# RWKV-7 block of a two-layer trunk: coupling, bonus and output products at other places of TensorE's fixed order, copies and small factors on ScalarE

## The chip, the core and the metric

The kernel runs on one core of a Trainium2 chip. The metric is the device time of one execution in microseconds (us), here the median over the runs shown. Five engines work side by side and are joined by semaphores: PE (TensorE, the matrix products), DVE (VectorE), ACT (ScalarE), POOL (GpSimd) and SP (SyncE, which only issues transfers). Each engine executes its own instructions strictly in the order in which they stand. An instruction that waits therefore holds up all that stand behind it on its engine, whether these wait for anything or not. This is the key to the whole change: nearly all it does is to alter such orders.

## What is computed

The reference is a trunk of two layers on x of 512 rows and 1024 columns, in f32. Each layer is half a SwiGLU feed-forward net, a mixer, and half a feed-forward net again. The mixer of layer 0 is attention and that of layer 1 is RWKV-7 time mixing, the only part that concerns us:

```python
xr, xw, xk, xv, xa, xg = [h + xx * mix[i] for i in range(6)]
r = (xr @ w_r).astype(f32)
k = (xk @ w_k).astype(f32)
v = (xv @ w_v).astype(f32)
...
def rwkv7_step(state, inp):
    r_t, w_t, k_t, v_t, a_t, b_t = inp
    sa = jnp.einsum('bhvk,bhk->bhv', state, a_t)
    state = (state * w_t[:, :, None, :] + sa[..., None] * b_t[:, :, None, :]
             + v_t[..., None] * k_t[:, :, None, :])
    return state, jnp.einsum('bhvk,bhk->bhv', state, r_t)
...
y = ((y - mu) * lax.rsqrt(var + GN_EPS)).reshape(B, S, D)
y = y * lnx_g.astype(f32) + lnx_b.astype(f32)
y = y + (jnp.sum(r_h * k_h * r_k.astype(f32), axis=-1, keepdims=True) * v_h).reshape(B, S, D)
return (y.astype(h.dtype) * g) @ w_o
```

There are 16 heads of 64 columns. The term with r_k is the "bonus": a sum over each head of r times k, spread over the head again and multiplied with v.

## The kernel before

**Products.** Every f32 operand of a large product is split into a high and a low part, and each product is made of three matmuls (mm3). All of them go through one helper line, L112 of the kernel, so that in the profile they are told apart by the tile they write: `rm` is a bank of the projections of k, v and r, `rq` a bank for small products (decay, coupling, sums over heads and their spread, transposes), `rr` and `ra` are the recurrence's, `wo` the output product's and `b` the feed-forward net's. These tiles lie in PSUM, from which an engine must have copied a bank before TensorE may fill it anew.

**The recurrence** does not step through time. The 512 positions fall into 8 chunks of 64, and within a chunk the steps are solved together, which needs the inverse of a triangular matrix for each head and chunk. The 16 heads are two groups of 8 ("group 0" and "group 1"). For each group `rw_own_ties` makes the products inside 32-position blocks, `rw_inverse` inverts these blocks, and its coupling steps (small 32x32 products) join two blocks to one of 64. Then `rw_recur` goes through the 8 chunks one after the other, each depending on the state that the last one left.

**The inverse** is a chain on VectorE: 31 pairs of a product and an add (L1376, L1380 before; L1379 and L1384 in the changed file), each over all blocks of the group at once. Its input `lin` is loaded from DRAM by SP; its result is copied by ScalarE (L1384 before, L1388 after, 128x1024, called "U" here) and goes with T out to DRAM (`tout`) and back in another layout, as the coupling steps need it.

**What sets the order.** A scheduler places the instructions of every engine, by costs and data, but inside the recurrent block `self.pinned` is set: each TensorE instruction is chained to the one before it, so TensorE follows the order in which the program writes them. That order is written out by hand. The functions are generators that stop ("yield") at places where other work may be put in, and `weave(main, (steps, side), ...)` goes through the main one and, after its n-th stop, takes one step of each side whose list names n. A projection `project` has 8 stops: after each of the first six k groups, then after each pair of banks with the last two k groups. `rw_recur` has 24, three for each chunk. Behind the block `pinned` is false and the scheduler places TensorE's instructions too; with `self.gate` an instruction can be put behind another in that order.

**Before**, the first half of r's projection carries the decay of group 1 in steps 0 to 3, the coupling of group 0's inverse in 2 to 5 and group 1's keys in 3 to 6. The second half carries the bonus sums (`rw_prep2`) and group 1's ties. The recurrence of group 0 carries the bonus sums of the second half (3, 4) and the coupling of inverse(1) (16, 17, 19, 20). The recurrence of group 1 carries the post-processing `rw_post(0)` of group 0, in which v is loaded back from DRAM (`vd`), transposed (L1567 on TensorE) and multiplied with the spread bonus; and the scheduler fills it with the output products of group 0's columns. `rw_post(1)` and the output products of group 1 follow, then the last feed-forward net.

## Time and profile before

| | us |
|---|---|
| three runs | 2158.67, 2158.33, 2158.3 |
| median | 2158.33 |
| the profiled execution | 2159.79 |
| its span | 2157.7 |
| recurrent block from r's projection to the last output product (timeline) | 1383 to 1794 |
| PE, DVE, ACT, POOL busy | 2071.5, 1166.8, 777.4, 168.1 |

The profile is one execution. Its own time stands 1.46 us over the median and 2.09 over its span, so sums made on the trace are brought to the median by taking off 1.46. In timeline rows the columns are start, duration, engine, line, operation, output and inputs, shapes, count, and in brackets how long the engine had been idle and what released it. A group of matmuls in one row is a run of them back to back. The granted clock is the share of full speed that TensorE was given, averaged over the stretch.

### The profile page before, as it was taken

The page shows a single profiled execution, that of the slowest core. Times are in us where ns is not written, and L with a number is a line of the kernel's source. Part 1 is how long each engine was busy: PE and PEld are TensorE (multiplying, and loading weights), DVE is VectorE, ACT ScalarE, POOL GpSimd, SP SyncE. Part 2 cuts the span into 40 slices and gives each one's busy share as a digit, 9 for nine tenths or more (in the row PEclk, how much of TensorE's full clock was granted, in tenths as well). Part 3 has the DMA queues.
Part 4 walks back from the last instruction along what each step waited for, and adds up shares of the span by engine and source line. Part 5 has one row for each costly group of instructions (what it writes and reads, how often), then busy time and mean ns, then how long its engine had stood idle before and what let it go on. Part 6 is the DMA issues. An engine that isn't in the chain of part 4 may idle for free.

```text
span 2157.7 us, 28358 instructions
## 1 busy us (share of the span) xinstructions
PE 2071.5 (96%) x11407; PEld 1665.8 (77%) x11407; DVE 1166.8 (54%) x1608; ACT 777.4 (36%) x1177; POOL 168.1 (8%) x193
## 2 busy tenths in 40 slices
PE   8999999999989999999999999998678989999999
PEld 6888887767878888888888888766456758888887
DVE  5444444367777544547445445676764545444443
ACT  4222223355335332335333333463314334222222
POOL 2000001011010000002000000123222101000000
PEclk9999999999989999999999999999799999999999
DMA  5232323331118656565554654447343332232331
GB/s 179 78 110 86 108 87 108 103 88 40 50 55 266 205 166 195 161 200 188 168 191 151 187 171 159 175 150 244 101 115 100 96 117 87 81 115 92 99 103 59
DMA packets 261915, 282.36 MB, mean 131 GB/s; under 512 B 45011, under 2 KB 221291, under 8 KB 261784
## 3 DMA queue, kind: packets, MB, share of 16 engines
q1 hardware_dynamic: 259672, 278.46, 41.7%
q10 hardware_dynamic: 2112, 2.10, 0.3%
q8 instruction: 89, 1.46, 0.3%
q14 instruction: 42, 0.34, 0.0%
HBM read 227.76 MB, written 54.59 MB: 131 GB/s over the span
## 4 chain that ended last, share of the span: by engine, by line
PE 90%; DVE 6%; DMA 2%; ACT 1%; issue 1%; SPq 0%; POOL 0%; ACTq 0%; DVEq 0%; POOLq 0%
PE b L112 67%; PE am L112 7%; PE rm L112 4%; PE rq L112 2%; PE wo L112 2%; PE rr L112 2%; PE rl L112 1%; DVE const L1376 1%; DVE const L1380 1%; DVE rec L873 1%; DMA parts<-parts 1%; PE an L695 0%; PE ad L852 0%; PE au L764 0%; DMA most<-const 0%
## 5 line engine op out<-in xcount | busy, mean ns | idle before, releaser
L112 PE MATMUL b<-xg,parts 128*128 128x512 f32 x4224 | 966.9, 390 | 0.7 <-ACT xg L395 0.7
L112 PEld LDWEIGHTS b<-xg,parts 128*128 128x128 f32 x4224 | 793.8, 188 | 168.0 <-issue 1.7
L268 DVE TENSOR_TENSOR parts<-const,parts 128x1024 fp32r<-128x1024 f32 (+1 forms) x320 | 362.8, 1141 | 303.0 <-ACT parts L267 302.4
L112 PE MATMUL b<-act,parts 128*128 128x512 f32 x2112 | 482.8, 389 | 0.0
L267 ACT CAST parts<-const 128x1024 fp32r<-128x1024 f32 (+1 forms) x320 | 312.1, 977 | 458.9 <-PE b L112 394.8
L112 PEld LDWEIGHTS b<-act,parts 128*128 128x128 f32 x2112 | 396.0, 188 | 82.1
L383 POOL TENSOR_TENSOR ssum<-ssum,sq 128x512 f32<-128x512 f32 x42 | 65.3, 1555 | 1205.6 <-DVE const L508 340.6
L508 DVE SCALAR_TENSOR_TENSOR const<-b,const 128x512 f32<-128x512 f32 x128 | 87.4, 687 | 107.5 <-PE b L112 107.5
L301 ACT CAST act<-u 128x512 fp32r<-128x512 f32 x88 | 54.7, 622 | 248.0 <-DVE u L494 248.0
L493 DVE TENSOR_TENSOR u<-b,rstd 128x512 f32<-128x512 f32 x88 | 60.5, 691 | 148.4 <-PE b L112 148.2
L94 ACT ACTIVATE g<-g 128x512 f32<-128x512 f32 x88 | 55.1, 630 | 189.7 <-DVE g L488 189.7
L488 DVE TENSOR_TENSOR g<-b,rstd 128x512 f32<-128x512 f32 x88 | 60.3, 689 | 94.9 <-PE b L112 94.6
L112 PE MATMUL am<-xg,parts 128*128 128x512 f32 x384 | 99.6, 411 | 0.2 <-ACT xg L395 0.2
L112 PEld LDWEIGHTS am<-xg,parts 128*128 128x128 f32 x384 | 72.4, 192 | 25.3 <-issue 9.4
L302 DVE TENSOR_TENSOR act<-u,act 128x512 fp32r<-128x512 f32 x88 | 60.6, 689 | 36.9 <-ACT act L301 36.4
L494 DVE TENSOR_TENSOR u<-u,g 128x512 f32<-128x512 f32 x88 | 60.5, 692 | 2.7
L112 PE MATMUL rm<-xm,parts 128*128 128x512 f32 x252 | 60.8, 394 | 0.0
L219 DVE TENSOR_TENSOR pparts<-praw,pparts 128x1024 fp32r<-128x1024 f32 (+2 forms) x37 | 42.9, 1163 | 29.1 <-ACT pparts L218 29.0
L112 PEld LDWEIGHTS rm<-xm,parts 128*128 128x128 f32 x252 | 46.6, 188 | 12.7 <-issue 3.2
L218 ACT CAST pparts<-praw 128x1024 fp32r<-128x1024 f32 (+2 forms) x37 | 36.9, 1003 | 53.3 <-DMA praw<-in_rw_wv_dram 13.0
L112 PE MATMUL wo<-z,parts 128*128 128x512 f32 x192 | 49.2, 401 | 2.2 <-ACT z L301 1.9
L112 PE MATMUL am<-parts,xg 128*128 128x512 f32 x192 | 47.5, 402 | 0.0
(261 smaller groups left out, 1729.2 us busy)
## 6 DMA issues: line engine op xcount, KB each, us to landing
const<-in_ffn_w_gate_dram SPq DMA_DIRECT2D x88, 512.0 KB
const<-in_ffn_w_up_dram SPq DMA_DIRECT2D x88, 512.0 KB
parts<-pparts SPq DMA_DIRECT2D x68, 512.0 KB
parts<-parts SPq DMA_DIRECT2D x68, 512.0 KB
const<-in_ffn_w_down_dram SPq DMA_DIRECT2D x64, 512.0 KB
const<-in_ffn_w_down_dram SPq DMA_DIRECT2D x48, 256.0 KB
const<-in_attn_w_in_dram SPq DMA_DIRECT2D x16, 512.0 KB
lora<-pparts SPq DMA_DIRECT2D x8, 576.0 KB
```

Of the source, the lines that this page charges most:

```text
L94: ins = nc.scalar.activation(out, in_, func, **kw)
L112: return self.pe(self.nc.tensor.matmul(*args, **kw))
L219: nc.vector.tensor_tensor(out=lo, in0=src, in1=hi.bitcast(F32), op=ALU.subtract)
L267: self.nc.scalar.copy(hi[:r, :n], raw[:, :n])
L268: self.lo_engine.tensor_tensor(out=lo[:r, :n], in0=raw[:, :n], in1=hi[:r, :n].bitcast(F32), op=ALU.subtract)
L301: self.nc.scalar.copy(hi, t)
L302: self.nc.vector.tensor_tensor(out=lo, in0=t, in1=hi.bitcast(F32), op=ALU.subtract)
L383: nc.gpsimd.tensor_tensor(out=ssum, in0=ssum, in1=sq, op=ALU.add)
L488: nc.vector.tensor_tensor(out=g, in0=ps[i], in1=rstd, op=ALU.mult)
L493: nc.vector.tensor_tensor(out=u, in0=ps[2 + i], in1=rstd, op=ALU.mult)
L494: nc.vector.tensor_tensor(out=u, in0=u, in1=gs[i], op=ALU.mult)
L508: nc.vector.scalar_tensor_tensor(out=self.x[c], in0=ps, scalar=0.5, in1=self.x[c], op0=ALU.mult, op1=ALU.add)
```

## The change

Six things are altered. (1) In r's projection the decay moves from steps 0 to 3 of the first half to 2 to 5, group 1's keys go to 6, 7 and, of the second half, 0, 1; the coupling of inverse(0) moves to steps 2 to 5 of the second half, the ties to 4 to 7, the bonus sums to 6, 7. (2) In the recurrence of group 0 the bonus sums move from 3, 4 to 6, 7 and the coupling of inverse(1) from 16, 17, 19, 20 to 18, 19, 21, 22. (3) The load of `vd`, its transposes and the bonus product leave `rw_post` for a generator of their own, `rw_bonus`; the recurrence of group 1 carries `rw_bonus(0)`, `rw_post(0)` and, in steps 15 to 19, `rw_bonus(1)`, which stood behind the recurrence before. (4) The output products of group 0 are put behind the last TensorE instruction of the recurrence of group 1. (5) r's four banks are copied to SBUF by ScalarE and VectorE reads the copies; the bank with the head sums is copied by ScalarE instead of VectorE. (6) Three kinds of small operations go from VectorE to ScalarE: the factor 1/C of the means of v (8 of 128x8), the addition of 1 in the decay (8 of 128x512), the factor -2 of each chunk's first column (8 of 128x8). The inverse's load from DRAM is no longer held back by the masks; its first VectorE operation is.

```diff
+        weave(project(0, None, evac_r, False, 0), ((2, 3, 4, 5), decay), ((6, 7), keys))
         weave(
-            project(0, None, evac_r, False, 0),
-            ((0, 1, 2, 3), decay), ((2, 3, 4, 5), inverse), ((3, 4, 5, 6), keys),
+            project(1, None, evac_r, False, 0),
+            ((0, 1), keys), ((2, 3, 4, 5), inverse), ((4, 5, 6, 7), ties), ((6, 7), bonus[0]),
         )
-        weave(project(1, None, evac_r, False, 0), ((0, 1), bonus[0]), ((0, 1, 2, 3), ties))
...
-        weave(recur, ((3, 4), bonus[1]), ((16, 17, 19, 20), inverse))
+        weave(recur, ((6, 7), bonus[1]), ((18, 19, 21, 22), inverse))
...
-        post = self.rw_post(0)
-        recur = self.rw_recur(1)
-        weave(recur, ((1, 2, 4, 5, 7, 8, 10, 11, 13, 14), post))
-        for _ in post:
-            pass
+        plus, post, more = self.rw_bonus(0), self.rw_post(0), self.rw_bonus(1)
+        weave(
+            self.rw_recur(1),
+            ((0, 2, 3, 4, 6), plus), ((1, 3, 4, 5, 7, 8, 10, 11, 13, 14), post), ((15, 16, 17, 18, 19), more),
+        )
+        done = self.last_pe
         self.pinned = False
         self.fetch_x(self.rr[1, 2])
-        self.rw_out(self.z)
+        self.rw_out(self.z, done)
...
-                nc.vector.tensor_scalar(out=mean, in0=mean, scalar1=1.0 / C, scalar2=None, op0=ALU.mult)
+                nc.scalar.mul(mean, mean, 1.0 / C)
...
-            nc.vector.tensor_scalar(out=pi, in0=pi, scalar1=1.0, scalar2=None, op0=ALU.add)
+            nc.scalar.activation(pi, pi, AF.Identity, bias=self.const(1.0))
...
-        for j, r in enumerate(rs):
+        rows = self.t("r", [4, S])
+        for j, ps in enumerate(rs):
+            nc.scalar.copy(rows[:, j, :], ps)
+        for j in range(4):
             m = 4 * sg + j
-            t, rp = rw["k"][m], self.plane(sg, j, 1)
+            t, r, rp = rw["k"][m], rows[:, j, :], self.plane(sg, j, 1)
...
-            nc.vector.tensor_copy(y, ps)
+            nc.scalar.copy(y, ps)
...
-        load = self.after(nc.sync.dma_start(L, rw["lin", sg]), dep)
+        load = nc.sync.dma_start(L, rw["lin", sg])
...
+            if i == 0:
+                self.after(ins, dep)
...
+    def rw_bonus(self, sg):
+        nc = self.nc
+        self.plus = [self.plane(0, j, 4) for j in range(4)]
+        vns = [self.plane(0, j, 1) for j in range(4)]
+        for j in range(4):
+            m = 4 * sg + j
+            src = self.rw["vd"][:, :, m * P : (m + 1) * P].rearrange("b p d -> p b d")
+            nc.sync.dma_start(vns[j].rearrange("p (b d) -> p b d", b=4), src)
+        yield
+        for j, (vn, t) in enumerate(zip(vns, self.plus)):
+            pv = self.bank("rq", 3)
+            for b in range(4):
+                self.pe(nc.tensor.transpose(pv[:, b * P : (b + 1) * P], vn[:, b * P : (b + 1) * P], self.ident))
+            nc.scalar.copy(t, pv)
+            pb = self.head_spread("b", 4 * sg + j)
+            nc.vector.tensor_tensor(out=t, in0=t, in1=pb, op=ALU.mult)
+            yield
...
-    def rw_out(self, z, late=4, dep=None):
+    def rw_out(self, z, dep=None):
         nc = self.nc
+        self.gate = dep
         for cb in range(4):
             w = self.next_w()
-            self.gate = dep if cb >= late else None
```

**TensorE, r's projection, around the first coupling step, before.** `rm` with 12 is one k group (or two banks of the last two k groups), `rq<-hids,parts` a decay piece, `rq<-const,heads 32x32` and `rq<-heads,const 32x32` the four coupling steps, `rq<-hids` the spread of a key norm.

```order
L112 MATMUL rm<-xm,parts 128x512 x12
L112 MATMUL rq<-hids,parts 128x512 x6
L112 MATMUL rm<-parts 128x512 x12
L112 MATMUL rq<-hids,parts 128x512 x6
L112 MATMUL rq<-const,heads 32x32 x32
L112 MATMUL rm<-parts 128x512 x12
L112 MATMUL rq<-hids,parts 128x512 x6
L112 MATMUL rq<-const,heads 32x32 x32
L112 MATMUL rq<-hids 128x512
L112 MATMUL rm<-xm,parts 128x512 x12
L112 MATMUL rq<-heads,const 32x32 x32
```

And in the change, where the rows begin with the end of the first half (its last two bank pairs with the first two spreads of keys) and lead into the second half; `rq<-heads 64x64` are the ties.

```order
L112 MATMUL rq<-hids 128x512
L112 MATMUL rm<-parts 128x512 x12
L112 MATMUL rq<-hids 128x512
L112 MATMUL rm<-parts 128x512 x12
L112 MATMUL rq<-hids 128x512
L112 MATMUL rm<-xm,parts 128x512 x12
L112 MATMUL rq<-const,heads 32x32 x32
L112 MATMUL rm<-parts 128x512 x12
L112 MATMUL rq<-const,heads 32x32 x32
L112 MATMUL rm<-parts 128x512 x12
L112 MATMUL rq<-heads,const 32x32 x32
L112 MATMUL rq<-heads 64x64 x16
```

The first coupling step stood behind the third k group of the first half; now it stands behind the third k group of the second half, with eight groups of rm products, four key spreads and a decay piece in between.

**ScalarE, the same place.** Before, the copy of the finished inverse (128x1024) stood between the last exponential of a decay piece and the coupling's copies:

```order
L94 ACTIVATE heads<-heads 128x512 x2
L1110 CAST xm<-const 128x512
L1292 ACTIVATE heads<-pa,const 128x512
L1384 COPY const<-const 128x1024
L1411 COPY const<-rq 32x512
L1110 CAST parts<-const 128x512
```

In the change, two pieces. The first is the decay: `heads<-rq` is a tanh that empties a bank, `heads<-heads 128x512 x2` are two exps that take in VectorE's scan.

```order
L94 ACTIVATE heads<-rq,const 128x512
L94 ACTIVATE pa<-rq,const 128x512
L1270 ACTIVATE heads<-heads,const 128x512
L1099 ACTIVATE const<-const 128x512
L94 ACTIVATE heads<-heads 128x512 x2
L1110 CAST parts<-const 128x512
L1110 CAST xm<-const 128x512
L94 ACTIVATE heads<-rq,const 128x512
```

The second is the copies of r's banks (L1338) with the copy of the inverse (L1388).

```order
L94 ACTIVATE heads<-heads 128x512 x2
L1338 COPY r<-rm 128x512
L1270 ACTIVATE heads<-heads,const 128x512
L1099 ACTIVATE const<-const 128x512
L1388 COPY const<-const 128x1024
L1338 COPY r<-rm 128x512
L1293 ACTIVATE heads<-pa,const 128x512
L1338 COPY r<-rm 128x512
L1110 CAST parts<-const 128x512
L1338 COPY r<-rm 128x512
```

One copy of a bank stands ahead of the inverse's copy, and three behind it.

**TensorE, the end of the recurrence of group 1, before.** `wo` are output products, `rr` and `ra` the recurrence, L1567 the transposes of v, `rq<-heads,const 8x512` sums over heads.

```order
L112 MATMUL rr<-recur,heads 64x64 x8
L112 MATMUL wo<-z,parts 128x512 x16
L112 MATMUL rr<-recur,heads 64x64 x8
L112 MATMUL wo<-z,parts 128x512 x21
L112 MATMUL rr<-am,bs 64x64 x8
L112 MATMUL rr<-heads,recur 64x64 x8
L112 MATMUL wo<-z,parts 128x512 x3
L112 MATMUL rq<-heads,const 8x512
L1567 MATMUL rq<-const,heads 128x128 x4
```

And in the change:

```order
L112 MATMUL rr<-recur,heads 64x64 x16
L112 MATMUL rr<-am,bs 64x64 x8
L112 MATMUL rr<-heads,recur 64x64 x8
L112 MATMUL wo<-z,parts 128x512 x24
L112 MATMUL rq<-heads,const 8x512 x4
L112 MATMUL rq<-hids,parts 128x512 x3
L112 MATMUL wo<-z,parts 128x512 x24
L112 MATMUL rq<-hids,parts 128x512
```

All output products now stand behind the recurrence, and group 1's sums stand between them; the transposes of v are gone from this place, into the recurrence.

More of the change, by code (lines that the diff above doesn't have):

```diff
@@ L1298, in rw_keys @@
             )
[L1299 to L1301 removed]
+            nc.scalar.mul(ar[:, 0, :, 0:1], ar[:, 0, :, 0:1], -2.0)
             nc.gpsimd.tensor_copy(self.pend[:, sg, j, :, None], ar[:, 1, :, C - 1 : C])
```

27 lines of the change are left out of this document (6 added, 21 removed).

## The prediction

> **What bounds the kernel now.** The page comes first: which engine fills the span, and where its row of slices dips.
>
> ```profile
> span 2157.7 us, 28358 instructions
> PE 2071.5 (96%) x11407; PEld 1665.8 (77%) x11407; DVE 1166.8 (54%) x1608; ACT 777.4 (36%) x1177; POOL 168.1 (8%) x193
> PE   8999999999989999999999999998678989999999
> PEclk9999999999989999999999999999799999999999
> ```
>
> TensorE is busy for 96% of the span. Its one long dip is slices 28 to 33, which is the recurrent block. So I cut that block at its own seams, read from TensorE's timeline further down, and asked for the engines' busy time in each piece (columns: length; busy time of PE, PEld, DVE, ACT, POOL; granted clock; DMA share; GB/s).
>
> ```profile
> 1380.00:1480.00 100.00, 100.00 (x526) 72.44 (x524) 64.05 (x96) 57.21 (x94) 22.35 (x22) 1.00 0.52 155
> 1491.37:1587.98 96.61, 68.72 (x613) 49.31 (x611) 70.22 (x123) 34.13 (x52) 28.72 (x25) 0.84 0.48 138
> 1587.98:1662.97 74.99, 53.99 (x1309) 43.88 (x1308) 42.29 (x96) 26.63 (x65) 13.38 (x17) 0.89 0.34 90
> 1662.97:1739.32 76.35, 73.30 (x1109) 54.29 (x1111) 37.29 (x55) 28.10 (x69) 11.65 (x12) 1.00 0.39 114
> 1739.32:1794.02 54.70, 45.50 (x182) 30.48 (x177) 29.65 (x42) 20.46 (x33) 7.31 (x6) 0.91 0.30 95
> ```
>
> The first row is a stretch ahead of the piece at stake, full to the brim. The other four are the projection of r (with decay, keys, inverse and ties woven in), the recurrence of group 0, the recurrence of group 1, and the tail with post-processing and output product. TensorE idles 27.9, 21.0, 3.05 and 9.2 us in them. The waits of TensorE name the causes (total, times, longest).
>
> ```profile
> PE rq L112 <- DMA const<-tout: 25.1, 2, 24.8
> PE rr L112 <- DVE rb L1351: 6.6, 1, 6.6
> PE rr L112 <- ACT const L1515: 5.6, 5, 3.9
> PE rm L112 <- DVE k L1342: 2.4, 2, 1.5
> ```
>
> The first is the inverse of group 0: a chain of 31 pairs of VectorE operations, then a copy, then a trip through DRAM. TensorE's fixed order puts its first coupling step before the rest of r's projection, so everything behind stands. TensorE's timeline:
>
> ```profile
> 1491.37 2.88 PE L112 MATMUL rm<-parts 128*128 128x512 f32 x12
> 1498.02 0.96 PE L112 MATMUL rq<-hids,parts 64*128 64x512 f32 x6
> 1498.91 3.01 PE L112 MATMUL rm<-parts 128*128 128x512 f32 x12
> 1527.66 0.28 PE L112 MATMUL rq<-const,heads 32*32 32x32 f32 x2 [24.84 <-DMA const<-tout]
> 1528.17 1.91 PE L112 MATMUL rq<-const,heads 32*32 32x32 f32 x62 [0.23 <-DMA const<-tout]
> 1530.01 4.52 PE L112 MATMUL rm<-parts 128*128 128x512 f32 x12
> 1535.34 1.20 PE L112 MATMUL rq<-const,heads 32*32 32x32 f32 x64
> 1541.01 0.50 PE L112 MATMUL rq<-hids 40*128 40x512 f32 x1
> 1587.98 1.10 PE L112 MATMUL ra<-heads 64*64 64x128 f32 x32
> 1632.62 1.97 PE L112 MATMUL rr<-const 128*64 128x64 f32 x32 [3.89 <-ACT const L1515]
> 1636.17 0.68 PE L112 MATMUL rr<-const 64*64 64x64 f32 x16
> 1641.82 0.68 PE L112 MATMUL rr<-const 64*64 64x64 f32 x16
> ```
>
> After the stall the first work is slow as well: 1.91 us against 1.20, and 4.52 against 3.01. Together 2.2 us.
>
> **Part 1, the projection.** The coupling steps move from the first half's steps 2 to 5 to the second half's. Behind 1491.37 TensorE now has, before the first coupling step: in the first half eight groups of twelve rm products (2.95 each, since 1498.91 less 1498.02 and the like give 3.0), four decay pieces (0.9), two key spreads (0.43); in the second half three more groups and two more spreads. That is 11 x 2.95 + 4 x 0.9 + 4 x 0.43 = 37.8 us, to 1529.2. VectorE and ScalarE rows for when the inverse is there:
>
> ```profile
> 1481.20 0.19 DVE L1376 TENSOR_TENSOR const<-const 128x31 f32<-128x31 f32 x1 [9.92 <-DMA const<-lin]
> 1509.83 0.41 DVE L1376 TENSOR_TENSOR const<-const 128x240 f32<-128x240 f32 x1
> 1521.73 0.19 DVE L1380 TENSOR_TENSOR const<-const 128x31 f32<-128x31 f32 x1
> 1521.96 1.93 ACT L1384 COPY const<-const 128x1024 f32<-128x1024 f32 x1 [5.71 <-DVE const L1380]
> 1530.77 0.68 DVE L1411 COPY const<-rq 32x512 f32<-32x512 f32 x1 [8.85 <-ACT const L1411]
> ```
>
> The inverse ends at 1521.92 and TensorE had it at 1527.66. The changed order keeps its first operation behind the same load and takes only four small multiplications and some adds out of its stretch, so I leave it there: 1528 against 1529, covered. The 25.1 us go, the waits for key products go (2.4), and with them nearly all of the 27.9 us idle in that piece; the 2.2 us of slow work go too: 30.1 us in all.
>
> What is late next is ScalarE's queue. (a) The second bank of the third decay piece needs the first tanh of the second to have emptied a bank. In ScalarE's new order that tanh stands behind two exps, which wait for VectorE's scan of the first piece, which stands behind 20 pairs of the inverse. The 20th pair stood at 1509.83; two scans of 1.22, two adds and the four multiplications leave the stretch ahead of it, so about 1508 now. Then 1.2 scan, 1.15 exps, 1.2 for two casts, 0.7: 1512.3, against 1508.4 at which TensorE is there. Stall 3.9. (b) r's four banks are now emptied by ScalarE, and the copy of the finished inverse (1.93, waits for its end) stands ahead of three of them. So they come at 1525.0, 1526.4 and 1527.6 with an exponential and a cast between, while TensorE, by (a), opens the second half at 1523.2. I take 3, between 2 and 4. (c) A mix cast of the fourth k group waits for VectorE behind the inverse: 2.7 by the same walk. Together about 9.5, bounds 0 and 15. **Term: 9.5 - 30.1 = -20.6 us.**
>
> **Part 2, recurrence of group 0.** Its idle 21.0 us hang on inverse(1), and that on the end of the projection:
>
> ```profile
> 1589.82 0.42 SPq L1367 DMA_DIRECT2D const<-lin  x1
> 1598.45 0.19 DVE L1376 TENSOR_TENSOR const<-const 128x31 f32<-128x31 f32 x1 [7.74 <-issue]
> 1629.57 0.19 DVE L1380 TENSOR_TENSOR const<-const 128x31 f32<-128x31 f32 x1
> 1629.84 1.95 ACT L1384 COPY const<-const 128x1024 f32<-128x1024 f32 x1 [2.27 <-DVE const L1380]
> ```
>
> Load, 8.6 us until VectorE starts, 31.3 us of chain, and the rows of the recurrence that stand in between on VectorE: all move along with the projection's end. Moving the coupling from steps 16 to 20 to 18 to 22 cannot help, as TensorE stands ahead of them already (1632.62). The copy for the sums (0.7) leaves VectorE. Against it: in ScalarE's order the copy of the inverse, 1.95, now has that same copy, its cast and one recurrence copy (0.67 + 0.62 + 0.4) right behind it and ahead of what TensorE waits for, where before only L1515 followed. That costs 3.8 by the walk. **Term: +3.1.** Bounds 0 and +5.
>
> **Part 3, recurrence of group 1.** 93 products of the output leave it; one row gives their price, and the chain of waits shows what stands in the tail:
>
> ```profile
> 1733.41 4.99 PE wo L112 x21
> 1739.32 4.36 DMA heads<-vd
> 1743.81 0.63 PE rq L1567 x4
> 1744.44 4.81 PE rq L112 x7
> 1754.92 2.79 PE rq L112 x5
> 1771.51 6.64 PE wo L112 x28
> 1794.02 6.12 PE b L112 x27
> ```
>
> 4.99 / 21 = 0.24 us, so 93 x 0.24 = 22.3 us go. Four transposes (0.6 each by the row of 0.63) and four spreads (0.43) of group 1 come in: 4.1. Of the 73.3 busy us 55.1 remain. Without products to fill, the recurrence waits for its own ScalarE copies: a chunk without filler took 1641.82 - 1636.17 = 5.65 us, of which 4.6 busy. One us for each of eight chunks would be 8; filler still stands in seven of them, so I take 4 (bounds 2 and 8). 59 us against 76.35. **Term: -17.3.**
>
> **Part 4, the tail.** The 93 products land here, the 4.1 us leave. Before, it idled 9.2 us and lost some 3 us to the slower clock (0.91): the load of vd (4.36), and the chain from the sums at 1744.44 to the spread at 1754.92. In the change 96 ready products, 23 us, stand around that chain, which took 27 us from 1744.44 to 1771.51 with TensorE's part in it. I leave 3 us of waiting for the last z (bounds 0 and 6). 22.3 - 4.1 - 9.2 + 3 - 3 = **+9.0.**
>
> **The ScalarE moves.** Groups of instructions by shape (busy, mean ns; idle before):
>
> ```profile
> L1272 DVE TENSOR_TENSOR_SCAN heads<-const,heads 128x512 f32<-128x512 f32 x8 | 9.8, 1222 | 0.2
> L94 ACT ACTIVATE heads<-heads 128x512 f32<-128x512 f32 x16 | 9.2, 623 | 10.1 <-DVE heads L1272 10.0
> L1133 ACT COPY v<-rm 128x512 f32<-128x512 f32 x8 | 4.6, 582 | 8.0 <-PE rm L112 8.0
> L1504 ACT COPY recur<-rr 128x256 f32<-128x256 f32 x16 | 6.0, 372 | 10.3 <-PE rr L112 9.9
> ```
>
> Sixteen small factors, eight adds, eight copies of r's banks and two of sums join ScalarE. Sixteen at 0.37 or less and eighteen at 0.58 to 0.62 make some 17 us. In the stretch where TensorE is full (first windows row) ScalarE is busy 57 us of 100, and only a few of them fall there. Taken at 0, bounds -1 and +2; where they lie inside (a) to (c) they are counted.
>
> **Sum.** -20.6 + 3.1 - 17.3 + 9.0 = -25.8. The profiled execution took 2159.79 us, 1.46 above the median of 2158.33. So 2134.0 there, **2132.5 against the median**.
>
> **A rule set against this.** The rows show granted clocks of 0.84 and 0.89 where TensorE stalls for long, and 1.00 in group 1's recurrence, whose gaps stay under 1.2 us. The Trainium skill, "TensorE: Matmul & The Clock Gate", section "A second HAM failure mode: psum-queue depth-cycling", says that many micro-idles between groups of matmuls make the clock swing to half. That speaks against part 3, which makes such gaps. By it the stage could run at half speed throughout, an estimate of 55 us more, 2187; by the row of unfilled chunks, below, nothing.
>
> **Rivals.**
> 1. *No new stall.* ScalarE gets through, 9.5 and 3.8 us do not arise: 2132.5 - 13.3 = **2119**. For it: ScalarE is busy 34 of 97 us in the projection. Against it: it is a queue, and the waits in it are on VectorE at its fullest. 0.2.
> 2. *VectorE takes over.* It is busy 70 of 97 us in the projection, and idle after the inverse for 8.85 us only. If the key products and mixes behind the inverse set the pace, only that idle time is gained: -8.9 + 3.1 - 17.3 + 9.0 = -14.1, **2144**. 0.2.
> 3. *The stall merely moves.* If tout comes as late after TensorE's arrival as before, part 1 gives nothing: -5.2, **2153**. It would need the inverse 25 us later than 1522. 0.05.
> 4. *Slower: group 1's recurrence loses its clock.* Its 55.1 busy us at 0.65, the lowest mean in a stretch of the stalled stage, become 84.8, +29.7: **2162**. It decides from a clock of about 0.67 downward over the whole stage. The last row below, unfilled chunks with gaps of half a microsecond, speaks against it. 0.05.
>
> ```profile
> 1500.00:1520.00 20.00, 2.82 (x15) 1.75 (x13) 19.25 (x39) 9.62 (x16) 4.88 (x6) 0.65 0.26 95
> 1640.00:1660.00 20.00, 18.63 (x615) 16.18 (x611) 6.85 (x12) 10.07 (x25) 4.35 (x5) 1.00 0.32 80
> ```
>
> My forecast has the rest, 0.5. All but the fourth are faster than before by over 0.2% (4 us, about what a measurement of this kernel can tell from no change). With a little kept for what I have not seen: faster 0.88, within 0.2% 0.06, slower 0.06. The range takes in rivals 1 and 2 with the bounds of the terms: 2117 to 2149.
>
> **What would show it.** Right: no wait on tout above 2 us, project to coupling without a hole; short waits of TensorE on ScalarE rows (the tanh, the r copies) of 2 to 4 us around 1508 and 1524; the recurrence of group 1 near 59 us with clock 1.00; the tail near 64 us. Wrong: a wait on tout of 10 us or more (rival 3), the rm products waiting on VectorE's key products for over 8 us (rival 2), no ScalarE wait at all (rival 1), a clock below 0.9 in group 1's recurrence (rival 4).

## The result: 18 us faster, three tenths less than forecast

The changed kernel takes 2140.24 us in the median of four runs (2139.44 to 2140.55), the kernel before 2158.32 in runs beside it. The ratio is 0.9917, with a 95% interval of 0.99 to 0.9935. Forecast were 2132.5 us with a range of 2117 to 2149. The direction was right and the time lies in the range, but of 25.8 us only 18.1 came, and the runs below show that a part of these came from a place that the prediction had not looked at.

The page after, in the rows that answer to those of before:

```profile
span 2138.5 us, 28350 instructions
PE 2073.1 (97%) x11407; PEld 1668.3 (78%) x11407; DVE 1163.9 (54%) x1582; ACT 789.0 (37%) x1211; POOL 167.9 (8%) x194
PE   8999999999989999999999999999788899999999
PEclk9999999999999999999999999999888999999999
```

The dip is shallower, but it is still there. The same four pieces, cut at the same events to within 0.3 us (length; busy PE, PEld, DVE, ACT, POOL; granted clock; DMA share; GB/s):

```profile
1488.05:1570.96 82.91, 70.62 (x613) 49.31 (x611) 74.92 (x113) 41.90 (x73) 32.25 (x25) 0.92 0.59 173
1570.96:1648.54 77.58, 59.00 (x1310) 48.27 (x1309) 40.17 (x93) 29.26 (x69) 13.49 (x17) 0.81 0.32 84
1648.54:1713.44 64.90, 57.62 (x1042) 42.29 (x1041) 33.17 (x52) 29.25 (x72) 10.68 (x12) 0.97 0.32 93
1713.44:1774.62 61.18, 59.63 (x245) 44.04 (x243) 31.72 (x45) 18.17 (x29) 7.14 (x6) 1.00 0.37 121
```

| piece | before | after | change | forecast |
|---|---|---|---|---|
| r's projection | 96.61 | 82.91 | -13.7 | -20.6 |
| recurrence of group 0 | 74.99 | 77.58 | +2.6 | +3.1 |
| recurrence of group 1 | 76.35 | 64.90 | -11.5 | -17.3 |
| tail | 54.70 | 61.18 | +6.5 | +9.0 |
| ahead of the block (starts at 1491.37, now 1488.05) | | | -3.3 | 0 |
| sum | | | -19.4 | -25.8 |

The four pieces give 16.1 us. Over them TensorE's idle time falls by 21.4 us (from 61.1 to 39.7), but its busy time grows by 5.4 (from 241.5 to 246.9) for nearly the same products (3213 and 3210): part of what is won in waits is lost again in slower products. The 3.3 us ahead of them were not forecast at all: TensorE begins the projection of k already 5.95 us earlier (1377.66 against 1383.61; the 1383 in the table ahead of the prediction is this start, while r's projection begins at 1491.37), though up to there no engine's order differs but for one constant more on GpSimd. It loses 2.6 of these again, 2.1 of them to weights that come late. What TensorE waits for in the block now (total, times, longest):

```profile
PE rr L112 <- DVE const L1457: 10.4, 5, 4.5
PE rr L112 <- ACT recur L1508: 4.9, 5, 2.7
PE rq L112 <- ACT heads L94: 4.8, 2, 3.7
PE rm L112 <- POOL parts L1112: 4.0, 1, 4.0
PE rm L112 <- DMA parts<-parts: 3.3, 5, 1.2
PE rq L112 <- DVE hids L302: 2.7, 1, 2.7
PE rm L112 <- ACT parts L1110: 1.3, 1, 1.3
PE rm L112 <- ACT r L1338: 0.9, 2, 0.7
```

The wait on tout, 24.8 us in one piece, is gone. A dozen short ones stand in its place. In TensorE's timeline and ScalarE's they look like this:

```profile
1511.26 1.64 PE L112 MATMUL rq<-hids,parts 64*128 64x512 f32 x5 [3.69 <-ACT heads L94]
1512.84 4.62 PE L112 MATMUL rm<-parts 128*128 128x512 f32 x12
1536.59 1.20 PE L112 MATMUL rq<-const,heads 32*32 32x32 f32 x64
1543.65 4.34 PE L112 MATMUL rm<-parts 128*128 128x512 f32 x11 [4.04 <-POOL parts L1112]
1613.87 1.01 PE L112 MATMUL rr<-recur,heads 64*64 64x64 f32 x14 [2.69 <-ACT recur L1508]
...
1508.45 1.15 ACT L94 ACTIVATE heads<-heads 128x512 f32<-128x512 f32 x2 [3.47 <-DVE heads L1273]
1510.53 0.68 ACT L94 ACTIVATE heads<-rq,const 128x512 f32<-128x512 f32 x1
1524.03 2.08 ACT L1388 COPY const<-const 128x1024 f32<-128x1024 f32 x1
1525.98 0.61 ACT L1338 COPY r<-rm 128x512 f32<-128x512 f32 x1
...
1539.13 6.15 POOL L1112 TENSOR_TENSOR parts<-const,parts 128x512 fp32r<-128x512 f32 x2 [5.31 <-ACT parts L1110]
```

Row by row these are the three waits that the prediction had worked out. (a) The tanh at 1510.53 stands behind the two exps that waited 3.47 us for the scan: TensorE waits 3.69. (b) The copy of the inverse at 1524.03 stands ahead of the copies of r. (c) The fourth k group of the second half waits for its mix, the last 4 us of it for GpSimd, whose two subtractions took 6.15 us. The coupling itself (1536.59) waits for nothing.

### The profile page after: what moved, and what is told of

Same layout as the page of the kernel before. It is cut to its first block, busy times and chain, and to the rows that moved or that the text cites. A ratio compares the mean times of both kernels' runs of the same rounds, so it can differ in the third digit from the quotient of the medians.

```text
span 2138.5 us, 28350 instructions
## 1 busy us (share of the span) xinstructions
PE 2073.1 (97%) x11407; PEld 1668.3 (78%) x11407; DVE 1163.9 (54%) x1582; ACT 789.0 (37%) x1211; POOL 167.9 (8%) x194
## 3 DMA queue, kind: packets, MB, share of 16 engines
q8 instruction: 89, 1.46, 0.3%
## 4 chain that ended last, share of the span: by engine, by line
PE 90%; DVE 5%; DMA 2%; ACT 1%; issue 1%; POOL 0%; SPq 0%; ACTq 0%; POOLq 0%; DVEq 0%
PE b L112 67%; PE am L112 7%; PE rm L112 4%; PE rq L112 2%; PE wo L112 2%; PE rr L112 2%; PE rl L112 1%; DVE const L1378 1%; DVE const L1384 1%; DVE rec L873 1%; PE an L695 1%; PE au L764 0%; DMA most<-const 0%; PE ad L852 0%; PE ra L112 0%
## 5 line engine op out<-in xcount | busy, mean ns | idle before, releaser
L383 POOL TENSOR_TENSOR ssum<-ssum,sq 128x512 f32<-128x512 f32 x42 | 63.5, 1512 | 1198.1 <-ACT sq L382 462.8
L302 DVE TENSOR_TENSOR act<-u,act 128x512 fp32r<-128x512 f32 x88 | 60.5, 689 | 36.9 <-ACT act L301 36.5
L112 PE MATMUL rm<-parts,xm 128*128 128x512 f32 x192 | 47.3, 398 | 2.1 <-DMA parts<-parts 2.1
L112 PE MATMUL wo<-z,parts 128*128 128x512 f32 x192 | 46.5, 393 | 1.6 <-ACT z L301 0.8
```

What stands on the lines that cost most here:

```text
L112: return self.pe(self.nc.tensor.matmul(*args, **kw))
L302: self.nc.vector.tensor_tensor(out=lo, in0=t, in1=hi.bitcast(F32), op=ALU.subtract)
L383: nc.gpsimd.tensor_tensor(out=ssum, in0=ssum, in1=sq, op=ALU.add)
```

## The experiments

Chips differ a little (the kernel before has medians of 2156.45 to 2158.32 us on them), and so do the early parts of single executions. So beside the medians and ratios, which are against the kernel before on the same chip, I read each profile from one fixed event, the end of the last tie product of group 0 ("tie"), where the block's work at stake begins. In the table: from there to the first product of group 0's recurrence; from there to the end of the second inverse on VectorE; from the end of that inverse to the start of group 1's recurrence; that recurrence; the tail (all us); the time and the ratio.

| kernel | tie to recurrence 0 | tie to end of inverse 1 | from there to recurrence 1 | recurrence 1 | tail | median | ratio |
|---|---|---|---|---|---|---|---|
| before | 121.8 | 163.6 | 33.2 | 76.7 | 54.4 | 2158.3 | 1 |
| constant added | 123.9 | 163.8 | 34.3 | 76.6 | 52.6 | 2153.2 | 0.9981 |
| ScalarE's moves alone | 119.3 | 158.7 | 34.9 | 75.8 | 54.2 | 2150.4 | 0.9967 |
| order alone | 117.7 | 154.1 | 37.9 | 67.0 | 61.3 | 2146.4 | 0.9944 |
| projection's order as before | 119.3 | 150.3 | 41.9 | 64.9 | 61.3 | 2143.2 | 0.9934 |
| the change | 110.8 | 148.7 | 39.7 | 65.0 | 61.3 | 2140.2 | 0.9917 |
| the change, second chip | 110.3 | 148.2 | 38.9 | 65.1 | 61.3 | 2139.2 | 0.9916 |
| output products ungated | 110.4 | 151.5 | 38.9 | 79.8 | 52.8 | 2144.2 | 0.9939 |
| inverse copied by GpSimd | 113.0 | 149.9 | 40.6 | 65.0 | 61.3 | 2139.6 | 0.9915 |
| decay spread | 111.5 | 149.2 | 37.5 | 65.3 | 61.3 | 2138.2 | 0.9912 |
| ties before coupling | 110.7 | 142.9 | 39.0 | 65.1 | 61.3 | 2133.1 | 0.9877 |
| second inverse longer | 111.2 | 155.6 | 35.8 | 65.3 | 61.3 | 2142.5 | 0.9924 |
| ties first, inverse not held | 108.2 | 143.4 | 46.5 | 63.5 | 61.3 | 2140.1 | 0.9912 |
| the same, decay spread | 110.8 | 142.1 | 43.6 | 66.5 | 61.9 | 2140.2 | 0.9913 |

### Where the 6 us ahead of the block come from

```diff
+            self.const(1.0)
             nc.vector.tensor_scalar(out=pi, in0=pi, scalar1=1.0, scalar2=None, op0=ALU.add)
```

> The kernel before with one thing added: the one-column constant 1.0 of the change is created at the same place and never used. No instruction of the block moves. In the profile of the change TensorE reaches r's projection some 3 us earlier than before, and already at the start of the projections of k it is 6 us earlier, although the order of all engines is the same up to there. Theory 'placing': the constant shifts what lies behind it and the early part runs differently; then this kernel is 3 to 6 us faster than before, 2152 to 2155, with the first product of the k projection near 1377.7 us instead of 1383.6. Rival 'chance': the early part differs from build to build or from execution to execution for other reasons; then 2158 and 1383.6.

Measured: 2153.16 us, ratio 0.9981 (0.997 to 0.9992), and the first product of k's projection at 1376.07. An unused constant makes the kernel 4 us faster. The profile shows a place where this comes about, at the start of attention, where GpSimd makes the last sum of squares for TensorE. Before, and with the constant:

```profile
375.79 0.62 ACT L382 ACTIVATE sq<-const 128x512 f32<-128x512 f32 x1
376.76 0.17 DVE L922 TENSOR_SCALAR const<-const 128x48 f32<-128x48 f32 x1
376.92 3.11 POOL L383 TENSOR_TENSOR ssum<-ssum,sq 128x512 f32<-128x512 f32 x1 [1.82 <-ACT sq L382]
380.08 2.08 PE L422 MATMUL b<-ssum,const 128*128 128x512 f32 x2 [2.27 <-POOL ssum L383]
```

```profile
375.10 0.62 ACT L382 ACTIVATE sq<-const 128x512 f32<-128x512 f32 x1
376.07 1.26 DVE L922 TENSOR_SCALAR const<-const 128x48 f32<-128x48 f32 x1
375.87 1.28 POOL L383 TENSOR_TENSOR ssum<-ssum,sq 128x512 f32<-128x512 f32 x1 [1.46 <-ACT sq L382]
377.20 1.13 PE L422 MATMUL b<-ssum,const 128*128 128x512 f32 x2
```

GpSimd begins 0.5 us after the square without the constant, 0.15 us with it. Where it is ahead of VectorE's small operation, it is through in 1.28 us and VectorE's operation takes 1.26 instead of 0.17; where it is behind, it takes 3.11, and TensorE waits 2.3 us for it and then runs slowly (2.08 us for two products instead of 1.13). The two kernels without the constant (before, and the order alone) show this wait, all others do not. Set side by side product by product, the twelve profiles with the constant gain 4.2 to 5.9 us on that of before between 370 and 395 us, and the order alone gains nothing there. So 'placing' holds; why one more memset lets GpSimd begin 0.36 us earlier is not settled. In the change this gift is in the 18 us. A second shift, between 590 and 680 us, is not the constant's: there all profiles gain 0.9 to 3.3 us on the one of before, the order alone 2.8. It goes with the one profile of the kernel before, which stands 1.46 us over its median, and makes up the rest of the 5.95 us.

### Which part carries the gain

Order alone: all moves to ScalarE undone, as in

```diff
-            nc.scalar.activation(pi, pi, AF.Identity, bias=self.const(1.0))
+            nc.vector.tensor_scalar(out=pi, in0=pi, scalar1=1.0, scalar2=None, op0=ALU.add)
```

> The change without its moves to ScalarE: r's banks are read by VectorE from PSUM again, the sums' copy, the factors 1/C and -2 and the addition of 1 are VectorE's. The new places in TensorE's order stay. Theory: the gain is the order's, and the ScalarE queue gives a little back; the waits on the r copies (0.9 us) go, the wait on the tanh (4.8 us) stays, since it hangs on the scan behind the inverse: 2138 to 2144. Rival 'ScalarE carries it': without the relief VectorE sets the pace of the projection and half of the gain or more is lost: 2149 or more.

Measured: 2146.37 us, 0.9944 (0.9923 to 0.9964). It lies between the two theories, 6 to 7 us above the change. The constant's 4 us are missing, and in its profile, an execution of 2149.3 us and so 3 over the median, some 6 us more in the block (402.8 us from the k projection to the last output product, against 397.1 and 395.9 in the two profiles of the change). TensorE's waits here begin with VectorE's masks at 13.4 us and tout, again, at 10.2: without the relief the first inverse takes 65.5 us from its first to its last operation (45.1 in the change), since more of VectorE's other work stands between its steps, and the cover is too short.

ScalarE's moves alone, the reverse:

> The kernel before with the moves to ScalarE alone (r's banks, sums, factors 1/C and -2, the addition of 1 with its constant); TensorE's order is untouched. Theory: it has the constant's 4 us, and from the ties of group 0 to the recurrence of group 1 it saves the 5.5 us that the change with the old projection order saved there (192.2 us against 197.7), so 2146 to 2150. Rival 'the moves are free of effect, it was the bonus work moved elsewhere': only the constant's gain, 2152 to 2155.

Measured: 2150.39 us, 0.9967 (0.9953 to 0.9981), 0.4 us above the upper end of the first theory: by the ratios some 3 us less than the constant alone, with intervals that overlap. They shorten the way to the end of the second inverse by 5 us (158.7 against 163.8), and TensorE still waits 22.6 us for tout. By the ratios the constant (4 us), ScalarE's other moves (3) and the order with the gate, the bonus and the freed load (12) add up to 19 us, against 18 for the change.

The projection's order as before, all else as in the change:

```diff
-        weave(project(0, None, evac_r, False, 0), ((2, 3, 4, 5), decay), ((6, 7), keys))
         weave(
-            project(1, None, evac_r, False, 0),
-            ((0, 1), keys), ((2, 3, 4, 5), inverse), ((4, 5, 6, 7), ties), ((6, 7), bonus[0]),
+            project(0, None, evac_r, False, 0),
+            ((0, 1, 2, 3), decay), ((2, 3, 4, 5), inverse), ((3, 4, 5, 6), keys),
         )
+        weave(project(1, None, evac_r, False, 0), ((0, 1), bonus[0]), ((0, 1, 2, 3), ties))
```

> The change with the order of r's projection as it was before (decay 0 to 3, coupling 2 to 5, keys 3 to 6 in the first half; bonus sums 0, 1 and ties 0 to 3 in the second); all else as in the change. Theory: the long wait on tout comes back, 25 us, and the short ScalarE waits there go; the projection takes 95 to 97 us instead of 82.9, and what follows only moves along: 2152 to 2155. Rival: the wait on tout is paid somewhere else in any case (the second inverse sets the end of group 0's recurrence), and the time stays within 5 us of the change: 2140 to 2145.

My theory fell here. The time is 2143.23 us, 0.9934 (0.9917 to 0.995), 3 to 4 us more than the change (the intervals overlap; the two profiles of the change are 3.8 and 5.0 us shorter from the k projection to the last output product), though the long wait is back:

```profile
PE rq L112 <- DMA const<-tout: 22.6, 2, 22.4
PE rr L112 <- DVE const L1457: 7.4, 5, 5.0
PE rr L112 <- ACT const L1519: 6.4, 6, 4.3
```

TensorE reaches the recurrence of group 0 8.5 us later than in the change. But the second inverse ends only 1.6 us later (150.3 against 148.7). The stall of 25 us was not the bound: TensorE waits in any case, there or in the recurrence of group 0, while VectorE makes the second inverse. It does so through VectorE's order. The masks (L1457) and the state updates (L1527) of the early chunks stand there among the pairs of that inverse; in the change half of the eight chunks have their masks ahead of its end, and this update comes right behind it:

```profile
1608.62 0.19 DVE L1384 TENSOR_TENSOR const<-const 128x31 f32<-128x31 f32 x1
1608.73 0.42 DVE L1527 TENSOR_TENSOR recur<-rr,recur 128x256 f32<-128x256 f32 x1
1609.21 0.80 PE L112 MATMUL rr<-recur,heads 64*64 64x64 f32 x10 [1.38 <-DVE recur L1527]
```

With the old order its ties came early, its input was there sooner, and it began 3.3 us after TensorE's projection, which ended at 1577.51:

```profile
1580.78 0.18 DVE L1378 TENSOR_TENSOR const<-const 128x31 f32<-128x31 f32 x1
```

In the change the projection ends at 1570.96, and the inverse begins 9.1 us after it, at 1580.03, with VectorE idle for 5.70 us before it (its row stands further down).

The early input has a second reason, the last sentence of the change: the load of `lin` is no longer held back by the masks. With ScalarE's moves alone, where it still is, it starts 1.3 us after the projection's end (1577.70), and in the old-order run 3.5 us ahead of it (1577.51):

```profile
1578.97 0.50 SPq L1368 DMA_DIRECT2D const<-lin  x1
1574.01 0.34 SPq L1369 DMA_DIRECT2D const<-lin  x1
```

The second inverse begins 8.5 us after the projection in the first and 3.3 in the second. The two kernels differ in more than the load, and no run frees the load alone, so its share is not measured.

### The output products

```diff
-        self.rw_out(self.z, done)
+        self.rw_out(self.z)
```

> The change with the output products of group 0 free to be placed inside the recurrence of group 1 again. Theory: moving the products is neutral in work, and the gain of the change's place is the idle time of the tail (9.2 before, 1.6 now) less the idle time that the bare recurrence shows (7.3 now, 3.05 before); so here the recurrence takes 20 us more, the tail some 17 us less: 2141 to 2146. Rival 'the gate is what pays': without it the tail idles as before and the recurrence does not improve: 2150. Rival 'the gate costs': products fill the gaps of the recurrence and the bonus work is out of the tail anyway: 2134 to 2138.

Measured: 2144.21 us, 0.9939 (0.9922 to 0.9956), in the theory's range, 4 us over the change by medians, with intervals that overlap. The recurrence takes 14.8 us more than in the change and the tail 8.5 less, not 20 and 17. The theory's account by idle time does not hold: of the net 6.4 us only 1.4 are idle time, and 5.1 are busy time for the same products (1285, and 1286 in the change). In the tail the wait on the sums' parts (L302) is back with 5.8 us in one piece, as in the kernel before (5.7), and the granted clock there is 0.87 instead of 1.00. The gate pays because the output products of group 0 cover the chain of group 1's sums, and more by the clock than by the idle time.

### The short waits

The inverse's copy on GpSimd:

```diff
-        nc.scalar.copy(big(U), T.rearrange("p t j -> p j t"))
+        nc.gpsimd.tensor_copy(big(U), T.rearrange("p t j -> p j t"))
```

> The change with the transposed copy of the inverse (128x1024) on GpSimd instead of ScalarE, both groups. Theory: in the recurrence of group 0 it was ScalarE's queue behind this copy that held TensorE, 3.8 us by the rows; without it the recurrence of group 0 takes 73 to 75 us instead of 77.6, and the copies of r's banks come 2 us earlier, which is worth the 0.9 us of waits on them: 2134 to 2138. Rival: GpSimd's queue becomes the late one (its subtractions of the mixes stand behind a copy of 3 to 6 us, and TensorE waits 4 us for one of them already), then the projection takes as much longer as is gained: 2140 to 2144.

Measured: 2139.63 us, 0.9915 (0.9894 to 0.9937), between the two ranges and the same as the change on that chip, so nothing is gained, as the rival had it. GpSimd takes 1.98 us for the second copy, not 3 to 6; ScalarE took 1.97 in the change. The profile (an execution of 2141.82 us) has the way to the recurrence of group 0 2.7 us longer than the change there (113.0 against 110.3), and that recurrence no shorter. The wait behind ScalarE's copy is gone, and this has come up a little later, on TensorE:

```profile
1619.87 0.44 PE L112 MATMUL rr<-const 64*64 64x64 f32 x2 [3.89 <-DMA const<-vcd]
```

and what stands ahead on SP's queue:

```profile
1613.00 0.51 SPq L1389 DMA_DIRECT2D uout<-const  x1
1616.16 1.13 SPq L1404 DMA_DIRECT2D heads<-uout  x2
1617.38 1.26 SPq L1439 DMA_DIRECT2D const<-vcd  x2
```

SP's queue holds the copy's way through DRAM too, and this load of v for the next chunk (`vcd`) stands behind it; in the change the load of `vcd` that follows the inverse is issued at 1612.85, ahead of the loads from `uout`.

Decay spread to steps 0, 2, 4, 6, keys to 7 and 0 to 2:

> The change with the decay pieces at steps 0, 2, 4 and 6 of the first half instead of 2 to 5, the keys at 7 and at 0 to 2 of the second. Theory: TensorE waits for the tanh because a piece came every 3.85 us while the tanh of the piece before stood behind two exps that wait for a scan behind 20 pairs of the inverse; with 6 us and more between pieces that wait (4.8 us, with 2.4 us of slow clock behind it) goes, and the scans are a few pairs earlier. The stretch from the ties of group 0 to the recurrence of group 0 takes 104 to 107 us instead of 110.8: 2133 to 2138. Rival 'VectorE sets the pace': the key products and mixes come no earlier, the wait only moves to the mix of the fourth k group, and the stretch stays at 109 to 112 us: 2139 to 2142.

Measured: 2138.16 us, 0.9912 (0.9892 to 0.9932), between the two ranges; the stretch decides for the rival. The wait on the tanh is gone, the copies of r now cost 3.9 us instead of 0.9, and the stretch to the recurrence of group 0 is 111.5 us. It moved.

The change itself beside these two:

> The change itself, unaltered, beside the others on their chip. Theory 'placing' (see the run with the unused constant): its early part is some 6 us shorter than that of the kernel before, with the first product of the k projection near 1376 us and no wait of TensorE on the sum of squares at 378 us; 2139 to 2143. Rival 'chance': the early part is as before, 1381 to 1384, and the time 2144 to 2147.

Measured: 2139.16 us, 0.9916 (0.9898 to 0.9934), k's projection at 1376.10, no wait on the sum of squares. 'Placing' again.

### VectorE's chain

The theory in place of the one that fell: the start of group 1's recurrence hangs on the second inverse on VectorE. It makes a forecast of its own: exchange two sides of the weave, so that the ties come first and the coupling, for which nobody waits yet, behind them.

```diff
-            ((0, 1), keys), ((2, 3, 4, 5), inverse), ((4, 5, 6, 7), ties), ((6, 7), bonus[0]),
+            ((0, 1), keys), ((2, 3, 4, 5), ties), ((4, 5, 6, 7), inverse), ((6, 7), bonus[0]),
```

> The change with the ties of group 1 and the coupling of group 0 exchanged in the second half of r's projection: ties at steps 2 to 5, coupling at 4 to 7. The amount of work in TensorE's order is the same. Theory 'VectorE's chain': what sets the start of group 1's recurrence is the end of the second inverse on VectorE, not TensorE's stall; its input is stored after the last tie and loaded again, and in the change VectorE begins it 9.1 us after the projection's last product, with the old projection order 3.3 us after it. Here the last tie comes 7 us earlier, so the second inverse begins 3 to 4 us after the projection and ends 5 to 6 us earlier, and that passes through to the end: 2133 to 2136, against 2139 to 2140 of the change. Rival 'TensorE': nothing is taken out of TensorE's order, so the time stays, 2138 to 2141.

Measured: 2133.13 us, 0.9877 (0.9861 to 0.9894). It beats the change by 6 to 7 us, with an interval that does not touch the change's on its second chip. First and last operation of the second inverse, here:

```profile
1573.37 0.18 DVE L1378 TENSOR_TENSOR const<-const 128x31 f32<-128x31 f32 x1
1602.15 0.19 DVE L1384 TENSOR_TENSOR const<-const 128x31 f32<-128x31 f32 x1
```

and in the change:

```profile
1580.03 0.19 DVE L1378 TENSOR_TENSOR const<-const 128x31 f32<-128x31 f32 x1 [5.70 <-issue]
1608.62 0.19 DVE L1384 TENSOR_TENSOR const<-const 128x31 f32<-128x31 f32 x1
```

TensorE's projection takes as long as before (110.7 us); it ends at 1570.09, and the inverse begins 3.3 us after that. All of the gain is in the second column of the table, 142.9 against 148.2 to 148.7, as forecast.

The opposite test, ten more products in the second inverse:

```diff
             if i == 0:
                 self.after(ins, dep)
+            if sg == 1 and i == 15:
+                for _ in range(10):
+                    nc.vector.tensor_tensor(
+                        out=pv, in0=L[:, i, j:, None].to_broadcast([P, n, j]),
+                        in1=T[:, i : i + 1, :j].to_broadcast([P, n, j]), op=ALU.mult,
+                    )
```

> The change with the second inverse lengthened: its product at i = 15 (0.42 us on VectorE) is computed ten times more, with the same result. Theory 'VectorE's chain': all of the 4.2 to 4.6 us passes to the end: 2143 to 2145. Rival: the recurrence of group 0 is held by ScalarE's and SP's queues as much as by the inverse, and the time grows by less than 1.5 us: 2139 to 2141.

Measured: 2142.49 us, 0.9924 (0.991 to 0.9939), between the two ranges: 2 to 3 us over the change by medians, with an interval that overlaps its interval, and 3.4 to 4.6 by the profiles (400.5 us from the k projection to the last output product, against 397.1 and 395.9). The inverse itself grew by 6.6 us (35.4 against 28.8), so a third to two thirds of it passes through, where the theory had all. In the profile 3 to 4 us were made good behind it: one state update of the recurrence, at 1611.51, now stands ahead of the inverse's end, where in the change it followed.

Then the hold taken off as well:

```diff
-        inverse = self.rw_inverse(1, self.masked)
+        inverse = self.rw_inverse(1, None)
```

> As the exchange of ties and coupling, and the second inverse no longer held behind the first chunk's masks on VectorE: it begins when its input has come. Theory 'VectorE's chain': the input lands some 11 us after the last tie, near the projection's last product, so the inverse begins 0 to 2 us after it instead of 3 to 4; and the copies of the head sums come behind the transposed copy on ScalarE less often: 2130 to 2134. Rival: the first chunk of the recurrence now waits for its masks behind inverse operations, and what is gained at the end is lost at the start: 2133 to 2137.

Measured: 2140.06 us, 0.9912 (0.9898 to 0.9927). The rival, and more than it had: the second inverse begins at 1568.84, but ends no earlier than with the exchange alone (143.4 us after the tie, 142.9 there), and the recurrence of group 0 stands at once:

```profile
1578.85 1.39 PE L112 MATMUL rr<-const 64*64 64x64 f32 x11 [9.99 <-DVE const L1457]
```

Its masks are VectorE's too, behind the inverse. From the end of the inverse to the recurrence of group 1 it is now 46.5 us instead of 39: the early chunks have to be made up. So two chains go through one engine, and the hold is worth 7 us here (2140.06 against 2133.13, intervals apart).

> The run before with the decay pieces spread to steps 0, 2, 4, 6 besides. Theory: the spread took the wait on the tanh away and was worth 1 us in its own run, because the second inverse set the end in any case; with that inverse earlier the projection counts again, 1 to 3 us more: 2129 to 2133. Rival: still the inverse alone, no difference to the run before: within 1 us of it.

Measured: 2140.15 us, 0.9913 (0.9898 to 0.9927), no difference to the run before, as the rival had it. The theory's 2129 to 2133 rested on a gain in the run before that did not come.

## Why the prediction was right, and where not

**The wait on tout is covered.** Right: the coupling came at 1536.59 without a wait on tout. TensorE's way there, put at 37.8 us and the new waits, took 48.5. (The difference that the prediction shows for a k group, 1498.91 less 1498.02, is that of a decay piece, 0.9; the 2.95 is right: 1494.84 to 1497.79 in the profile of the change, for twelve products.)

**The three new waits.** All three came where they were put: (a) at 1507.6, 4.8 us in two pieces against 3.9; (b) 0.9 against 3; (c) 5.3 (4.0 on GpSimd, 1.3 on the cast) against 2.7. Mis-sized is the term of 9.5. TensorE idles 12.3 us in the piece, 1.2 of them for late weights, and its 613 products take 4.1 us more than the 66.5 that were left without the slow work of before (70.62): the twelve behind the wait of 3.69 took 4.62 us instead of 3.0. The prediction had taken 2.2 us off for the slow work behind the old stall and had charged nothing for the slow work behind the new ones. Together 16.4 against 9.5, which is the 6.9 us between -20.6 and -13.7.

Of (c) a part was overlooked: GpSimd's two subtractions took 3.07 us each, where the same ones have a mean of 1.39 over the block of the kernel before. The Trainium skill, "GPSIMD Engine Reference", section "8. Key points", says that GpSimd shares its SBUF interfaces with VectorE. In the 6.2 us of the two subtractions (a row of the windows, columns as above) VectorE was busy for 6.14, and the trace agrees in so far; no run here shows that this is the reason:

```profile
1539.10:1545.30 6.20, 2.15 (x5) 1.54 (x6) 6.14 (x9) 1.34 (x2) 6.15 (x2) 0.59 0.22 76
```

**The deeper fault: what the stall was worth.** The step "the 25.1 us go" took a stall of TensorE for time of the program. The projection's order was worth 3 to 4 us (the run with the old order), not 20.6. Rival 2 named VectorE, and its 2144 us is nearer to the 2140.24 than the forecast, but it had the key products and mixes behind the first inverse as its means, and of such waits only the 5.3 us on mixes, (c), came. The runs show the second inverse instead: its beginning hangs on the last tie and on the masks, and the early chunks of group 0 wait for VectorE while it lasts. Part 2 said that "all move along with the projection's end", and it begins 9.1 us behind that end, against 10.5 before; but the reason is another. Part 2 still counted with the load held by the masks, which the change frees, and what holds the inverse in the change is the late place of the ties; with early ties it begins after 3.3. The end of that inverse comes 15 us earlier after the tie of group 0, and 13.3 us of this are there with the old order too.

**Recurrence of group 0.** +3.1 forecast, +2.6 measured, but by luck. The wait behind ScalarE's copies came in the place that was named (2.69 us), yet the idle time of the piece did not grow: it fell from 21.0 to 18.6 us, since a wait of 6.6 us of before is gone. Its products, one more than before, take 59.0 us instead of 54.0, with a granted clock of 0.81 instead of 0.89, and this the prediction did not have.

**Recurrence of group 1.** Mis-sized is the waiting: 4 us taken from bounds of 2 and 8, and 7.3 measured, near the upper bound. 2.68 of these are one wait for the parts of the sums (L302, at 1666.16), which the sum did not have; the short gaps are 4.6 together. Filler does not close these gaps: a chunk with 1.7 us of filler took 7.34 us (1677.92 to 1685.26) and idled 0.76, the one without before took 5.65 and idled 0.66 (it was busy for 4.99, not for 4.6 as the prediction has it). The remaining 2.5 us are busy time, 1.4 of them slow products behind the wait of 2.68.

**Tail.** +9.0 forecast, +6.5 measured. TensorE waits 1.5 us for the last z instead of 3, with a clock of 1.00 as assumed; the other 1.0 us is busy time, which grew by 14.1 us instead of 15.2.

**The clock in the bare recurrence.** Rival 4 did not come about: the clock's mean over the stage is 0.97. Nor did the rule of the Trainium skill, "TensorE: Matmul & The Clock Gate", section "A second HAM failure mode: psum-queue depth-cycling", that many micro-idles make the clock swing: gaps of 0.5 to 0.8 us leave it at 1.00 here. Only the wait of 2.68 us, which ends at 1666.16, shows in it:

```profile
1655.00:1675.00 20.00, 17.32 (x227) 10.95 (x225) 9.70 (x15) 7.30 (x17) 2.91 (x3) 0.91 0.33 97
1675.00:1695.00 20.00, 17.45 (x371) 13.39 (x361) 13.96 (x21) 8.10 (x21) 4.39 (x6) 1.00 0.37 110
```

The two rows have nearly the same idle time, 2.68 us in one gap and 2.55 in several, and only the first loses clock: in these rows it is the length of one gap that counts, not the sum.

**Right in part by luck.** Without the constant's gain of some 4 us the change would stand near 2144, still in the range, but farther from the forecast.

## What to carry to other kernels

A long stall of the busiest engine tells where it waits, not what it costs: follow the chain of the engine that it waits for to the next place where they meet, and ask what moves the end of that chain. When two pieces of work are exchanged in a fixed order, put first the one whose result goes the longest way to the next bottleneck (here the ties, through DRAM to the second inverse), not the one that waits the longest. And charge each new wait of some 3 us for the slow clock behind it as well as for itself: behind waits of 2.68, 3.69 and 4.04 us the next products lost another 1.4, 2.4 and 1.6 us here.

## What the runs showed of the hardware that I had not expected

A constant of one column that nobody reads made the kernel 4 us faster (2153.16 against 2157.62 us). In the profiles with it GpSimd is ahead of VectorE with one addition, 0.36 us sooner after its input in the run with the constant alone, and takes 1.28 us instead of 3.11; the products behind it come 4.2 to 5.9 us earlier. GpSimd's subtractions took 3.07 us instead of a mean of 1.39 while VectorE was full. A single wait of TensorE of 2.3 or 2.7 us was enough for slow products behind it (2.08 us for two instead of 1.13), while gaps of up to 0.8 us with the same sum were not. Changes of a few us in a kernel like this can therefore come from a place that was not touched, and a run with the inert part alone tells them apart.
